# Two-layer diffusion backbone on one core: experts taken in an order set on the chip, 512-wide down and output projections, one closing branch

## The chip, the core and the metric

One NeuronCore of a Trainium2 chip runs the whole program as one launch. TensorE multiplies (PE; its weight loads are PEld), VectorE (DVE) and ScalarE (ACT) do elementwise work, GpSimd (POOL) clears a few tiles, and SyncE (SP) issues every DMA. The metric is the device time of one execution in microseconds; lower is better.

## The reference

Two layers over 256 latent and 256 context tokens of width 1024, all in f32. Each layer normalizes, modulates and projects the tokens, runs three groups of heads (grouped-query attention, a short convolution, differential attention), concatenates them and applies one output projection with a gated residual. Then layer 0 has a dense SwiGLU of width 2816, and layer 1 a mixture of 8 SwiGLU experts of the same width, of which each latent token takes 2:

```python
logits = (h @ rw) + rb
top_v, top_i = lax.top_k(logits, TOP_K)          # 2 of 8
gates = jax.nn.softmax(top_v, axis=-1)
combine = sum(one_hot(top_i, 8) * gates[..., None], axis=-2)
for e in range(8):
    out = out + combine[..., e:e + 1] * swiglu(h, wg[e], wu[e], wd[e])
```

The output is the latent stream after layer 1. The sum over experts can be taken in any order. The weights of one expert are three f32 matrices of 1024 x 2816.

## The kernel before, in words

The program goes through six stages: a first projection, `mixer(0)`, `dense(0)`, `moe_consts` and `route_prep`, `mixer(1)`, `moe(1)`. Up to the experts, an f32 product is made of three fp32r products of a high and a low part (`mm3`, L165); `chunk` (L138) loads a weight block into one of six raw buffers, ACT writes the high part (L148) and DVE the low one (L153). A planner orders the instructions of each engine by priority and readiness; only `pin` and `issue_after` fix an order by hand. Therefore work that stands later in the program can fill gaps of work that stands earlier.

`wo_part` (L694) multiplies half of the output projection (rows 4 to 7 of the mixed heads). It takes the 1024 output columns in four blocks of 256 (`dc`); one PSUM bank of tag "mm" holds two token tiles of 128 next to each other, and `resid2` (L731) multiplies by the gate and adds to the residual. The other half, `tail` (L719), already takes 512 columns at a time.

`dense` (L738) takes the 2816 columns in groups of 10, 10 and 2 blocks of 128. After the gate and up products of a group, the down product (L797) runs: for the two groups of 10 it also takes four blocks of 256 output columns with two "mm" banks, and for the last group it uses `tail`. `side` (L747) takes steps of `ada_next`, a generator that sums the next layer's modulation on DVE from 512 KB loads (L203, L210): four steps ahead of most gate/up pairs, two ahead of each block `dc`, and all that are left ahead of the last group's tail.

`route` (L832) makes the logits, the rank of each expert for a token, the position of each token within its expert (`posm`), the gates (`comb`) and two numbers in `cnt`: the largest count of tokens, and a bit mask of the experts that have more than 64 tokens. `moe` (L903) then goes through experts 0 to 7 in this order. An expert has up to 96 token slots (`CAP`), in three tiles of 32. `gather` (L966) picks the tokens of one or two experts with a permutation made from `posm`; `gate_up` (L1022) and `down` (L1071) go over the 2816 columns in groups of 1024, 1024 and 768; the 32-column products sit side by side in the array (`quads`). The products for the third tile of 32 stand in `third(m)` (L1019), a branch that PE takes only where the mask has the bit of this expert. `spread` adds the expert's result to `acc`.

The weights come through a ring of 14 buffers of 1 MiB (`load`, L934). `plan` (L921) lists the loads: for each group 8 loads for gate and up, and 4 or 3 for the down rows of the group before. Each `fetch` hands out the oldest buffer and issues the next load, which waits until its buffer has been read. SP keeps eight semaphores for its loads, so that at most eight are under way.

After the last expert, `over` (L1169) holds the largest count. Two branches in a row (L1171) test whether it is above 96 and above 192; each body would handle further slots. With these inputs neither body runs.

Of the kernel before, what the change touches and what calls it, by code (L numbers as in the profile page):

```python
# [18 lines left out]
NL = 256  # L19
# [19 lines left out]
C_ID, C_S0, C_S1, C_RA, C_RC, C_UT, C_IO, C_TM, C_P2, C_N = 0, 128, 256, 384, 640, 768, 896, 1024, 1088, 1096  # L39


def build(tc, x, c, ctx, c_ctx, w_ada, b_ada, norm_mix, norm_ffn, w_in, w_out, a_q_gain, a_k_gain,
# [33 lines left out]
    cnt = base.tile([128, 2], I32, name="cnt")  # L76
# [328 lines left out]
    def mixer(l, fill=(), pre=(None, None)):  # L405
# [282 lines left out]
        def wo(s, ps, k, wh, wl, kk, a, b):  # L688
            for i in range(2):
                ts = slice((2 * s + i) * 128, (2 * s + i) * 128 + 128)  # L690
                mm3(ps[:, i * 256:i * 256 + 256], mTh[:, k, ts], mTl[:, k, ts], wh[:, kk], wl[:, kk],
                    i == 0 and a, i == 1 and b, True)

        def wo_part(k0, kn):  # L694
            for dc in range(4):
                acc = {s: bank("mm") for s in qs}
                wh, wl = chunk(krows(w_out[l], k0, kn, dc * 256, 256))
                for s in qs:
                    for kk in range(kn):
                        wo(s, acc[s], k0 + kk, wh, wl, kk, kk == 0, kk == kn - 1)  # L700
                for s in qs:
                    resid2(s, dc, acc[s].rearrange("p (t n) -> p t n", t=2))
# [16 lines left out]
    def tail(t, a, ws, tag=("mm", "mm")):  # L719
        for dh, wd in enumerate(ws):  # L720
            ps = bank(tag[dh])
            n = len(a) // len(wd)
            for kk, (ah, al) in enumerate(a):
                wh, wl = wd[kk // n]
                mm3(ps, ah, al, wh[:, kk % n], wl[:, kk % n], kk == 0, kk == len(a) - 1)
            tmp = hp.tile([128, 512], F32, name="rtmp", tag="sq", bufs=2)
            dsl = slice(dh * 512, dh * 512 + 512)
            dve.tensor_mul(tmp, ps, gb[:, t // 2, dsl])
            dve.tensor_add(X[t][:, dsl], X[t][:, dsl], tmp)

    def resid2(s, dc, ps):  # L731
        tmp = hp.tile([128, 2, 256], F32, name="rtmp", tag="sq", bufs=2)
        dsl = slice(dc * 256, dc * 256 + 256)
        for i in range(2):
            dve.tensor_mul(tmp[:, i], ps[:, i], gb[:, s, dsl])
            dve.tensor_add(X[2 * s + i][:, dsl], X[2 * s + i][:, dsl], tmp[:, i])

    def dense(l):  # L738
        wg, wu, wd = dense_w_gate[l // 2], dense_w_up[l // 2], dense_w_down[l // 2]
        with tc.tile_pool(name="dp", bufs=1, reuse_waits="tile") as dp:  # L740
# [14 lines left out]
            for gn in (10, 10, 2):  # L755
# [41 lines left out]
                for dc in range(4):  # L797
                    side(ST[2])
                    acc = [bank("mm") for _ in range(2)]
                    for fp in range((gn + 3) // 4):  # L800
                        fn = min(4, gn - 4 * fp)
                        wh, wl = chunk(krows(wd, f0 + 4 * fp, fn, dc * 256, 256))
                        for s in range(2):
                            for i in range(2):
                                ts = slice((2 * s + i) * 128, (2 * s + i) * 128 + 128)
                                for kk in range(fn):
                                    f = 4 * fp + kk
                                    mm3(acc[s][:, i * 256:i * 256 + 256], ath[f][:, ts], atl[f][:, ts], wh[:, kk], wl[:, kk],
                                        i == 0 and f == 0, i == 1 and f == gn - 1, True)
                    for s in range(2):  # L810
                        resid2(s, dc, acc[s].rearrange("p (t n) -> p t n", t=2))
# [20 lines left out]
    def route(l, xnh, xnl, rp, mark):  # L832
# [50 lines left out]
        dve.tensor_add(posm, ps[:, 0:16].rearrange("p (t e) -> p t e", t=2), un)  # L883
        for t in LAT:
            dve.scalar_tensor_tensor(xnl[:, t], X[t], rs[t], xnh[:, t].bitcast(F32), op0=OP.mult, op1=OP.subtract)
        mx = rp.tile([128, 2], F32, name="lmx")
# [9 lines left out]
        cf = rp.tile([128, 2], F32, name="cf")  # L896
        fl = rp.tile([128, NE], F32, name="fl")
        dve.scalar_tensor_tensor(fl, ps[:, 16:24], 64.0, KM[:, C_P2 - C_UT:C_P2 - C_UT + NE], op0=OP.is_gt, op1=OP.mult)
        dve.reduce_sum(cf[:, 1:2], fl, axis=AX.X)
        dve.reduce_max(cf[:, 0:1], ps[:, 16:24], axis=AX.X)  # L900
        dve.tensor_copy(cnt, cf)

    def moe(l):  # L903
# [17 lines left out]
        def plan():  # L921
            prev = None
            for e in range(NE):
                for g in range(3):
                    yield from up_rows(moe_w_gate[m, e], moe_w_up[m, e], g)
                    if prev:
                        yield from down_rows(moe_w_down[m, prev[0]], prev[1])
                    prev = e, g
            yield from down_rows(moe_w_down[m, prev[0]], prev[1])
# [24 lines left out]
        while len(queue) < NR:  # L954
            queue.append(load(next(todo)))

# [163 lines left out]
        def gathers(es_):  # L1120
            perm, gh = gather([col(posm, e) for e in es_], iota)
# [8 lines left out]
        gathers((0, 1))  # L1130
        units = []
        pend = aT = py = qT = None
        for e in range(NE):
            gh = where[e][2]
            for g in range(3):
                def mid(e=e, g=g):
# [8 lines left out]
                    if e % 2 == 1 and e < NE - 1 and g == 0:  # L1145
                        gathers((e + 1, e + 2))
# [9 lines left out]
                if pend:  # L1156
                    down(aT, pend[1], py, fetch, more[e - (pend[1] == 2)])
                    if pend[1] == 2:
                        ys = collect(py)
                        units += [(qT, col(comb, e - 1), ys, t, dh, "tp", e == 1) for dh in range(2) for t in LAT]  # L1160
# [5 lines left out]
        for i, (dh, t) in enumerate(((0, 0), (0, 1), (1, 0), (1, 1))):  # L1166
            spread(qT, col(comb, NE - 1), ys, t, dh, ("mm", "mm", "tp", "tp")[i], False, True)

        over = nc.values_load(cnt[0:1, 0:1], min_val=0, max_val=NL)  # L1169
        for rnd in range(1, (NL + CAP - 1) // CAP):  # L1170
            with tc.If(over > CAP * rnd):  # L1171
                io = mp.tile([128, CAP], F32, name="io", tag="io")
                dve.tensor_scalar(io, iota, float(CAP * rnd), None, op0=OP.add)
                with tc.For_i(0, NE, 1) as e:
                    pc = mp.tile([128, 2, 2], F32, name="pc", tag="pc", bufs=1)
                    dve.tensor_copy(pc[:, :, 0:1], posm[:, :, bass.ds(e, 1)])
                    dve.tensor_copy(pc[:, :, 1:2], comb[:, :, bass.ds(e, 1)])
                    perm, gh = gather([[pc[:, t, 0:1] for t in LAT]] * 2, io)
                    qT = permT(perm, 0)

                    def src(w):
                        return w[m, bass.ds(e, 1)].rearrange("o r n -> (o r) n")

                    def rows(parts):
                        it = iter(parts)
                        return lambda: load(next(it))

                    py = [bank("at"), y2]
                    for g in range(3):
                        sg = gate_up(gh[:, 0], g, rows(up_rows(src(moe_w_gate), src(moe_w_up), g)), None, lambda: None)  # L1190
                        down(turn(sg, g), g, py, rows(down_rows(src(moe_w_down), g)))
                    ys = collect(py)
                    for dh in range(2):
                        for t in LAT:
# [121 lines left out]
```

## Time and profile before

| | us |
|---|---|
| three runs | 1583.59, 1584.4, 1586.29 (median 1584.4) |
| profiled execution | 1584.25 |
| its span, first to last instruction | 1582.5 |
| PE busy / weight loads / DVE / ACT | 1486.6 / 994.2 / 700.1 / 486.1 |
| bytes read from HBM | 392.21 MB, 249 GB/s over the span |

The span is what the trace shows; the execution's own time is 1.75 us longer. PE is busy for 94% of the span, but this is an average over stages that have different limits. The span is cut into 40 slices of 39.6 us in one part of the page; the experts' stage begins near 870 us, in the 22nd of them counted from 0.

### The profile page before, as it was taken

How to read it: one execution, taken by the hardware profiler on the slowest of the kernel's cores; microseconds unless marked ns; L12 is line 12 of the kernel's file. 1: busy time of each engine (PE TensorE's matmuls, PEld its weight loads, DVE VectorE, ACT ScalarE, POOL GpSimd, SP SyncE). 2: the span in 40 equal slices, each digit the busy share in tenths (PEclk: the TensorE clock that was granted, in tenths of full speed). 3: DMA queues.
4: the chain of work that ended last, by engine and by line, in shares of the span. 5: the costliest groups of instructions: out<-in, count | busy, mean ns of one | idle time of the engine just before them, and what ended most of it. 6: DMA issues, size and time to landing. Idle time of an engine off the chain costs nothing. (4 is left out here: it accounts for less than half of the span.)

```text
span 1582.5 us, 31693 instructions
## 1 busy us (share of the span) xinstructions
PE 1486.6 (94%) x13286; PEld 994.2 (63%) x13286; DVE 700.1 (44%) x1670; ACT 486.1 (31%) x1067; POOL 2.9 (0%) x17
## 2 busy tenths in 40 slices
PE   8999999999999999999998999999988899999995
PEld 6987767887898889878877354444432344344343
DVE  4798745798377754378866012021202121020222
ACT  4576663533223231366773111010201010010101
POOL 0000000000000000000000000000000000000000
PEclk9999999999999999999998999999999999999997
DMA  9443324267256742324417999999999999999960
GB/s 322 144 133 108 108 67 134 69 200 224 69 169 213 261 135 87 107 64 132 126 41 280 415 416 415 415 416 403 417 407 416 405 416 406 417 373 399 399 242 30
DMA packets 175188, 395.64 MB, mean 250 GB/s; under 512 B 13840, under 2 KB 92588, under 8 KB 175024
## 3 DMA queue, kind: packets, MB, share of 16 engines
q1 hardware_dynamic: 175024, 393.30, 67.0%
q8 instruction: 122, 2.00, 0.5%
q14 instruction: 42, 0.34, 0.1%
HBM read 392.21 MB, written 1.05 MB: 249 GB/s over the span
## 5 line engine op out<-in xcount | busy, mean ns | idle before, releaser
L1005 PE MATMUL mm<-w,gh 128*32 128x512 f32 (+1 forms) x3072 | 327.5, 559 | 18.0 <-DMA w<-in_moe_w_up 13.3
L1005 PEld LDWEIGHTS mm<-w,gh 128*32 128x32 f32 x3072 | 102.8, 110 | 210.8 <-issue 185.1
L1005 PE MATMUL at<-w,aT 128*32 128x256 f32 x3520 | 202.4, 380 | 12.7 <-DMA w<-in_moe_w_down 8.8
L148 ACT CAST w<-w 128x512 fp32r<-128x512 f32 (+1 forms) x244 | 138.4, 605 | 204.9 <-PE mm L167 86.5
L153 DVE TENSOR_TENSOR w<-w 128x1024 fp32r<-128x1024 f32 (+1 forms) x122 | 144.7, 1186 | 92.6 <-ACT w L148 92.4
L1005 PEld LDWEIGHTS at<-w,aT 128*32 128x32 f32 x3520 | 118.9, 110 | 100.3 <-DMA w<-in_moe_w_down 19.4
L166 PE MATMUL mm<-w,hTh 128*128 128x256 f32 (+1 forms) x360 | 107.2, 299 | 3.0 <-ACT hTh L361 2.7
L167 PE MATMUL mm<-w,hTl 128*128 128x256 f32 (+1 forms) x360 | 107.0, 297 | 0.0
L168 PE MATMUL mm<-w,hTh 128*128 128x256 f32 (+1 forms) x360 | 106.5, 296 | 0.0
L166 PE MATMUL mm<-w,aTh 128*128 128x256 f32 (+1 forms) x336 | 97.4, 290 | 0.0
L167 PE MATMUL mm<-w,aTl 128*128 128x256 f32 (+1 forms) x336 | 96.9, 289 | 0.0
L168 PE MATMUL mm<-w,aTh 128*128 128x256 f32 (+1 forms) x336 | 96.7, 288 | 0.0
L1052 DVE COPY aT<-tp 128x256 f32<-128x256 f32 x16 | 6.8, 424 | 174.2 <-PE tp L1051 174.2
L1005 PE MATMUL av<-w,gh 128*32 128x512 f32 (+1 forms) x768 | 81.1, 557 | 0.0
L166 PEld LDWEIGHTS mm<-w,hTh 128*128 128x128 f32 x360 | 69.1, 192 | 7.7 <-ACT hTh L361 3.5
L167 PEld LDWEIGHTS mm<-w,hTl 128*128 128x128 f32 x360 | 69.3, 193 | 4.1 <-issue 2.0
L166 PE MATMUL at<-hTh,w 128*128 128x512 f32 (+1 forms) x192 | 71.3, 373 | 0.3 <-ACT hTh L361 0.3
L168 PEld LDWEIGHTS mm<-w,hTh 128*128 128x128 f32 x360 | 69.1, 192 | 3.8 <-issue 2.4
L167 PE MATMUL at<-hTh,w 128*128 128x512 f32 (+1 forms) x192 | 71.0, 371 | 0.0
L168 PE MATMUL at<-hTl,w 128*128 128x512 f32 (+1 forms) x192 | 71.0, 374 | 0.0
L1041 DVE TENSOR_TENSOR msg<-msg,av 128x256 f32<-128x256 f32 (+1 forms) x24 | 9.6, 399 | 137.5 <-ACT msg L1040 137.5
L1068 DVE COPY aT<-tp 64x256 f32<-64x256 f32 x8 | 3.4, 428 | 149.1 <-ACT aT L1066 149.1
(373 smaller groups left out, 2529.2 us busy)
## 6 DMA issues: line engine op xcount, KB each, us to landing
w<-in_moe_w_down SPq DMA_DIRECT2D x88, 1024.0 KB, 12.2
w<-in_moe_w_gate SPq DMA_DIRECT2D x128, 512.0 KB, 10.8
w<-in_moe_w_up SPq DMA_DIRECT2D x128, 512.0 KB, 10.2
araw<-in_w_ada SPq DMA_DIRECT2D x80, 512.0 KB, 4.3
w<-in_moe_w_gate SPq DMA_DIRECT2D x64, 384.0 KB, 7.9
w<-in_moe_w_up SPq DMA_DIRECT2D x64, 384.0 KB, 7.7
w<-in_w_in SPq DMA_DIRECT2D x36, 512.0 KB, 4.0
w<-in_dense_w_gate SPq DMA_DIRECT2D x22, 512.0 KB, 4.6
```

The costliest lines, as they stand in the source:

```text
L148: act.copy(h[:, sl], r[:, sl])
L153: dve.tensor_sub(lo[:, sl], r[:, sl], h[:, sl].bitcast(F32))
L166: pe.matmul(ps, ah, bh, start=start, stop=False, skip_group_check=shared)
L167: pe.matmul(ps, al, bh, start=False, stop=False, skip_group_check=shared)
L168: return pe.matmul(ps, ah, bl, start=False, stop=stop, skip_group_check=shared)
L1005: pin(pe.matmul(ps(q), lhsT, rhs(q), start=start, stop=stop, tile_position=(0, 32 * q), skip_group_check=True))
L1041: dve.tensor_mul(a, a, ps[t][:, n:2 * n])
L1052: (dve.tensor_copy if c0 else act.copy)(aT[:, c0:c1], pt[:, 0:c1 - c0])
L1068: (dve.tensor_copy, act.copy)[i % 2](at[64:128, 4 * i:hi], pv[64:128, 0:hi - 4 * i, :, 1])
```

## The change

1. `route` also ranks the experts by their count of tokens. 1000 is added to the count of expert 0, so that it has rank 0. Position p of the new order takes the expert whose rank is entry p of 0, 1, 7, 2, 6, 3, 5, 4. The ids, the counts, the positions and the gates are moved into this order with a one-hot matrix (`Pi`), and the bit mask follows it.
2. SP loads the seven ids of positions 1 to 7 into registers after the first 14 loads of the ring, and the addresses of all weight loads from position 1 on are made from them. Position 0 keeps its fixed address.
3. Tokens are gathered for positions (0), (1, 2), (3, 4), (5, 6), (7) rather than in four pairs.
4. `wo_part` and the dense down product of the groups of 10 take 512 output columns at a time, one PSUM bank for each token tile (tags "mm", "mm", "av", "ad"), two weight rows of 512 in a chunk, and `resid` on 512 columns.
5. The second closing branch stands inside the first one.

```diff
-                    yield from up_rows(moe_w_gate[m, e], moe_w_up[m, e], g)
+                    yield from up_rows(at_(moe_w_gate, e), at_(moe_w_up, e), g)
...
+        ids = [0]
+        def at_(w, e):
+            return w[m, 0] if e == 0 else w[m, bass.ds(ids[e], 1)].rearrange("o r n -> (o r) n")
...
         while len(queue) < NR:
             queue.append(load(next(todo)))
+        ids += [nc.values_load(cnt[0:1, 2 + p:3 + p], engines=[mybir.EngineType.SP], min_val=0, max_val=NE - 1)
+                for p in range(1, NE)]
...
+        C = rp.tile([128, NE], F32, name="C")
+        dve.tensor_add(C, ps[:, 16:24], kc(C_K0))
+        o, sl = C[:, None, :].to_broadcast([128, NE, NE]), C[:, :, None].to_broadcast([128, NE, NE])
+        dve.tensor_tensor(g2, o, sl, op=OP.is_gt)
+        dve.tensor_tensor(e2, o, sl, op=OP.is_equal)
+        dve.tensor_mul(e2, e2, TM)
+        dve.tensor_add(g2, g2, e2)
+        dve.reduce_sum(rk, g2, axis=AX.X)
+        dve.tensor_tensor(Pi, rk[:, None, :].to_broadcast([128, NE, NE]), kc(C_OR)[:, :, None].to_broadcast([128, NE, NE]),
+                          op=OP.is_equal)
+        def moved(dst, src):
+            tmp = rp.tile([128, NE, NE], F32, name="tmp", tag="tmp", bufs=2)
+            dve.tensor_mul(tmp, Pi, src[:, None, :].to_broadcast([128, NE, NE]))
+            dve.reduce_sum(dst, tmp, axis=AX.X)
...
+        moved(cf[:, 2:2 + NE], kc(C_EI))
+        dve.tensor_copy(fl, ps[:, 16:24])
+        moved(c2, fl)
+        dve.scalar_tensor_tensor(fl, c2, 64.0, kc(C_P2), op0=OP.is_gt, op1=OP.mult)
...
+        for t in LAT:
+            moved(posm2[:, t], posm[:, t])
...
+        for t in LAT:
+            moved(comb2[:, t], comb[:, t])
...
+    K[:, C_OR:C_OR + NE] = np.array([0, 1, 7, 2, 6, 3, 5, 4])[None]
...
-        gathers((0, 1))
+        gathers((0,))
...
-                    if e % 2 == 1 and e < NE - 1 and g == 0:
-                        gathers((e + 1, e + 2))
+                    if e % 2 == 0 and e < NE - 1 and g == (1 if e == 0 else 0):
+                        gathers((e + 1, e + 2) if e + 2 < NE else (e + 1,))
...
-                for dc in range(4):
+                for dh in range(2):
                     side(ST[2])
-                    acc = [bank("mm") for _ in range(2)]
-                    for fp in range((gn + 3) // 4):
-                        fn = min(4, gn - 4 * fp)
-                        wh, wl = chunk(krows(wd, f0 + 4 * fp, fn, dc * 256, 256))
...
+                    acc = [bank(tag) for tag in ("mm", "mm", "av", "ad")]
+                    for fp in range(gn // 2):
+                        wh, wl = chunk(krows(wd, f0 + 2 * fp, 2, dh * 512, 512))
+                        for t in range(4):
+                            ts = slice(t * 128, t * 128 + 128)
+                            for kk in range(2):
+                                f = 2 * fp + kk
+                                mm3(acc[t], ath[f][:, ts], atl[f][:, ts], wh[:, kk], wl[:, kk], f == 0, f == gn - 1)
+                    for t in range(4):
+                        resid(t, dh, acc[t])
...
+            for dh in range(2):
+                acc = [bank(tag) for tag in ("mm", "mm", "av", "ad")[0:len(qt)]]
+                for kp in range(kn // 2):
+                    wh, wl = chunk(krows(w_out[l], k0 + 2 * kp, 2, dh * 512, 512))
...
+    def resid(t, dh, ps):
+        tmp = hp.tile([128, 512], F32, name="rtmp", tag="sq", bufs=2)
+        dsl = slice(dh * 512, dh * 512 + 512)
+        dve.tensor_mul(tmp, ps, gb[:, t // 2, dsl])
+        dve.tensor_add(X[t][:, dsl], X[t][:, dsl], tmp)
...
-        for rnd in range(1, (NL + CAP - 1) // CAP):
-            with tc.If(over > CAP * rnd):
...
+        with tc.If(over > CAP):
+            further(1)
+            with tc.If(over > 2 * CAP):
+                further(2)
```

## Rows read from the trace of the kernel before

**Rows 1.** The page: bytes moved by DMA, in 40 slices of the span.
```profile
GB/s 322 144 133 108 108 67 134 69 200 224 69 169 213 261 135 87 107 64 132 126 41 280 415 416 415 415 416 403 417 407 416 405 416 406 417 373 399 399 242 30
```

**Rows 2.** Stretches: span, busy us (instructions) by engine, clock, DMA share, GB/s.
```profile
870.00:930.20 60.20, 57.11 (x656) 25.25 (x659) 5.18 (x13) 6.62 (x14) 0.15 (x1) 1.00 1.03 415
930.20:1025.70 95.50, 93.57 (x1127) 45.16 (x1123) 14.84 (x34) 11.23 (x27) 0.15 (x1) 1.00 1.03 416
1025.70:1096.40 70.70, 67.07 (x820) 31.85 (x813) 12.21 (x26) 9.18 (x23) 0.15 (x1) 1.00 1.02 409
1096.40:1180.60 84.20, 72.36 (x805) 31.30 (x803) 14.84 (x34) 11.23 (x27) 0.15 (x1) 1.00 1.02 412
1180.60:1265.00 84.40, 69.33 (x769) 26.76 (x769) 12.22 (x26) 9.19 (x23) 0.15 (x1) 1.00 1.02 411
1265.00:1362.60 97.60, 94.22 (x1124) 43.34 (x1128) 14.12 (x30) 11.23 (x27) 0.15 (x1) 1.00 1.03 412
1362.60:1459.00 96.40, 93.45 (x1144) 40.04 (x1140) 12.21 (x26) 10.35 (x25) 0.15 (x1) 1.00 0.99 392
1459.00:1561.00 102.00, 100.36 (x1290) 44.63 (x1282) 18.69 (x36) 10.85 (x28) 0.15 (x1) 1.00 0.69 268
```

**Rows 3.** The same stretches, instructions on tile av alone (PE, PEld, DVE, ACT).
```profile
930.20:1025.70 95.50, 20.63 (x192) 7.27 (x192) 1.20 (x3) 1.10 (x3) 1.00 1.03 416
1096.40:1180.60 84.20, 0.00 (x0) 0.00 (x0) 1.20 (x3) 1.10 (x3) 1.00 1.02 412
```

**Rows 4.** The chain that ended last: start us, us, what; its last products.
```profile
1552.92 8.04 PE at L1005 x144
```

**Rows 5.** Timeline of SP: start us, us, engine, line, what.
```profile
552.62 5.90 SPq L203 DMA_DIRECT2D araw<-in_w_ada  x2
...
873.40 0.33 SPq L941 DMA_DIRECT2D w<-in_moe_w_up  x1
877.25 0.33 SPq L941 DMA_DIRECT2D w<-in_moe_w_gate  x1
...
1510.23 17.69 SPq L941 DMA_DIRECT2D w<-in_moe_w_down  x7
```

**Rows 6.** DMA issues: what, count, KB each, median us from issue to landing.
```profile
w<-in_moe_w_gate SPq DMA_DIRECT2D x128, 512.0 KB, 10.8
...
araw<-in_w_ada SPq DMA_DIRECT2D x80, 512.0 KB, 4.3
```

**Rows 7.** The closing branches (line 1171): count, ns min/median/max, first and last start.
```profile
L1171 SPq EVENT_SEMAPHORE  x16: 17/17/17, 1573.8 to 1581.1; - x16
...
L1171 PEldq COMPARE_BRANCH  x2: 4285/4690/5094, 1566.4 to 1570.9; - x2
...
L1171 SPq COMPARE_BRANCH  x2: 50/52/53, 1570.8 to 1576.0; - x2
```

**Rows 8.** Stretches as in Rows 2: down products 256 wide, gate/up products 512 wide.
```profile
588.90:646.40 57.50, 57.50 (x481) 57.50 (x480) 23.23 (x40) 12.93 (x25) 0.00 (x0) 1.00 0.32 94
545.40:588.90 43.50, 43.50 (x194) 36.02 (x192) 25.32 (x32) 14.56 (x27) 0.00 (x0) 1.00 0.49 160
```

**Rows 9.** Groups by line: count, busy us, mean ns; a 512-wide eviction on DVE.
```profile
L728 DVE TENSOR_TENSOR rtmp<-mm,gb 128x512 f32<-128x512 f32 x14 | 9.5, 685 | 2.4 <-PE mm L168 2.3
```

**Rows 10.** Timeline of DVE, then of PE, at the end of the routing.
```profile
862.65 0.16 DVE L901 CAST cnt<-cf 128x2 int32<-128x2 f32 x1
862.72 1.34 DVE L972 TENSOR_SCALAR perm<-KM,posm 128x96 fp32r<-128x96 f32 x7
...
863.87 0.50 PE L982 MATMUL tp<-perm,xnh 128*128 128x192 f32 x1 [2.31 <-DVE perm L972]
...
870.03 7.07 PE L1005 MATMUL mm<-w,gh 128*32 128x512 f32 x64
```

**Rows 11.** SP loading one value of cnt into a register at line 1169 (ns).
```profile
L1169 SPq TENSOR_LOAD <-cnt x1: 478/478/478, 1528.0 to 1528.0; - x1
L1169 SPq FUSED_REGOPS  x1: 183/183/183, 1528.5 to 1528.5; - x1
```

More of the change, by code (lines that the diff above doesn't have):

```diff
@@ L75, in build @@
     comb = base.tile([128, 2, NE], F32, name="comb")
[L76 removed]
+    cnt = base.tile([128, 2 + NE], I32, name="cnt")
+    posm2 = base.tile([128, 2, NE], F32, name="posm2")
+    comb2 = base.tile([128, 2, NE], F32, name="comb2")
     hps = ExitStack()
@@ L725, in tail @@
                 mm3(ps, ah, al, wh[:, kk % n], wl[:, kk % n], kk == 0, kk == len(a) - 1)
[L726 to L736, printed above, removed]
+            resid(t, dh, ps)
+    def resid(t, dh, ps):
[3 more added lines that the diff above has]
+        dve.tensor_add(X[t][:, dsl], X[t][:, dsl], tmp)
     def dense(l):
@@ L1120, in gathers @@
         def gathers(es_):
-            perm, gh = gather([col(posm, e) for e in es_], iota)
+            perm, gh = gather([col(posm2 if e else posm, e) for e in es_], iota)
             for i, e in enumerate(es_):
@@ L1166, in moe @@
         for i, (dh, t) in enumerate(((0, 0), (0, 1), (1, 0), (1, 1))):
-            spread(qT, col(comb, NE - 1), ys, t, dh, ("mm", "mm", "tp", "tp")[i], False, True)
+            spread(qT, col(comb2, NE - 1), ys, t, dh, ("mm", "mm", "tp", "tp")[i], False, True)
         over = nc.values_load(cnt[0:1, 0:1], min_val=0, max_val=NL)
-        for rnd in range(1, (NL + CAP - 1) // CAP):
-            with tc.If(over > CAP * rnd):
[L1172 to L1194, printed above, removed]
-                            spread(qT, [pc[:, t, 1:2] for t in LAT], ys, t, dh, "tp", False, True)
@@ new lines, in further, with src, rows @@
+        def further(rnd):
+            io = mp.tile([128, CAP], F32, name="io", tag="io")
+            dve.tensor_scalar(io, iota, float(CAP * rnd), None, op0=OP.add)
+            with tc.For_i(0, NE, 1) as e:
+                pc = mp.tile([128, 2, 2], F32, name="pc", tag="pc", bufs=1)
+                dve.tensor_copy(pc[:, :, 0:1], posm[:, :, bass.ds(e, 1)])
+                dve.tensor_copy(pc[:, :, 1:2], comb[:, :, bass.ds(e, 1)])
+                perm, gh = gather([[pc[:, t, 0:1] for t in LAT]] * 2, io)
+                qT = permT(perm, 0)
+                def src(w):
+                    return w[m, bass.ds(e, 1)].rearrange("o r n -> (o r) n")
+                def rows(parts):
+                    it = iter(parts)
+                    return lambda: load(next(it))
+                py = [bank("at"), y2]
+                for g in range(3):
+                    sg = gate_up(gh[:, 0], g, rows(up_rows(src(moe_w_gate), src(moe_w_up), g)), None, lambda: None)
+                    down(turn(sg, g), g, py, rows(down_rows(src(moe_w_down), g)))
+                ys = collect(py)
+                for dh in range(2):
+                    for t in LAT:
+                        spread(qT, [pc[:, t, 1:2] for t in LAT], ys, t, dh, "tp", False, True)
```

56 lines of the change are left out of this document (24 added, 32 removed).

## The prediction

> **What bounds the kernel now.** I read the page's DMA line first [rows 1]: up to slice 20 little is moved, from slice 22 on some 415 GB/s nearly without a pause, and only the last slices fall. So the experts' stage, 690 of 1582.5 us, streams weights, and the question is where the stream waits for PE and where PE waits for the stream. For that I cut the stage at the first gate/up product of each expert [rows 2] and asked the same stretches for the tile of the third 32 slots [rows 3]. The reader is to see two kinds of experts. Those with over 1100 PE products have the third tile run (192 products on "av"): 1, 5, 6 and 7, so these have more than 64 tokens. Call them big; 0, 2, 3, 4 are small. Two small ones in a row (3 and 4) take 84.2 and 84.4 us with PE busy for 72.4 and 69.3 at most: the stream sets their time, 84.3 us an expert. The big ones take 95.5 to 102 us with PE busy nearly throughout: PE sets theirs. In the order 0 to 7 the kernel pays for both kinds apart: at 1265 PE has used up every buffer, and then three big experts follow, in which the ring of 14 fills, the stream slows to 392 and 268 GB/s, and its last loads are issued by 1528 [rows 5], while PE works until 1552.92 + 8.04 = 1561.0 [rows 4]. After that come the last evictions, the output and 10 us of closing branches [rows 7].
>
> **The order of experts.** Expert 0 is small and first. Of the other seven, ranks 1 to 4 by count are the big ones 1, 5, 6, 7 in some order, and ranks 5 to 7 the small ones. The table 0, 1, 7, 2, 6, 3, 5, 4 therefore gives small, big, small, big, small, big, small, big, whatever the exact counts. Both partners of such a pair are in the trace already: experts 1 and 2, a big one after a small one and a small one after a big one, with one gather of two experts, took 95.5 + 70.7 = 166.2 us while the stream ran at 416 and 409 GB/s [rows 2]. The stream needs 84.2 + 84.4 = 168.6 for a pair. So PE and stream are level in each pair, and the stream barely bounds it. Position 7 starts, counted from the end of position 0, at 930.2 + 3 x 168.6 = 1436.0 by the stream and at 930.2 + 3 x 166.2 = 1428.8 by PE, to which the gather of positions 1 and 2 is added, since it moves into position 0 (under 6.2 us, from the first gather product to the first weight product [rows 10], half of that at full clock). Counted from the moment in the old run when the stream was the bound, 1265.0 + 168.6 = 1433.6. I take the mean of the stream's two values, 1434.8. Position 7 is big: 102.0 us in the old run, less the third tile in the last down products of the expert ahead of it, which is now small (48 of 144 products in 8.04 us, 2.7 [rows 4]): 99.3. PE ends at 1534.1 instead of 1561.0: 26.9 us gained. The ends are 33 (PE alone, 1428.8) and 18, if near-level pairs stutter by 3 us each.
>
> **The start of the experts.** The ranking puts about 20 small DVE instructions (seven up to `Pi`, two for each of six `moved`, one copy) ahead of the first `perm`, if the planner keeps program order. By the copy of `cnt` and the spacing of `perm` (0.16 and 1.34 / 7 = 0.19 us [rows 10]) that is 3.8 us; behind the waiting first gather products stand PE's mask load and all weight products. Only two `perm` and half the gather columns are needed now, which gives back between nothing and 3 us. So PE starts 0.8 to 4 us late. Does the stream notice? SP issues its last free load at 873.40 and the next one at 877.25, when PE has read the first half [rows 5]; a load lands 10.8 us after its issue [rows 6], so a release that is 4 us late still finds loads under way. The seven register loads sit in the same gap: 7 x (0.478 + 0.183) = 4.6 us [rows 11], from 873.7 to 878.3, 1.1 us past the old issue and ahead of the late one; queued behind them are only loads that wait for PE anyway, and 10 us of loads are in flight. I price the whole start at +1.5 us; its ends are 0 and 6.
>
> **The closing branch.** PE's two branches at the end take 4.3 and 5.1 us [rows 7], and SP, which carries the end, goes through its own branch at 1570.8 and 1576.0 and a row of eight semaphores after each, the last at 1581.1. Nested, the second is skipped with the first body: 1581.1 - 1576.0 = 5.1 us less, with nothing late in its place but the output, which lands during the first. Ends: 4.3 and 5.3. [...]
>
> **The 512-wide products.** A down product of 256 columns takes 57.50 / 480 = 0.1198 us, a product of 512 columns 43.50 / 192 = 0.2266 [rows 8], both with PE never idle. Two narrow ones become a wide one: 0.2396 - 0.2266 = 0.0130 us saved each. The dense groups of 10 have 480 such pairs (2 groups x 4 blocks x 10 rows x 4 token tiles x 3 products, halved): 6.2 us. `wo_part` of layer 0 has 96 pairs, of which a quarter fills waits of the attention: 72 x 0.0130 = 0.9. In layer 1 there are 48, most of them in such waits: 0.2. Chunks keep their size of 1024 columns and feed 24 products of 0.2266 = 5.4 us, so loads and casts stay hidden. Evictions: a tile's product with the gate takes 0.685 us [rows 9], and PE comes back to its bank after three other tiles, 3 x 6 x 0.2266 = 4.1 us; hidden, unless DVE is held up. If that cover fails at the four changes of block, up to 1.5 us each, 6 in all. The banks "av" and "ad" are shared with attention and the modulation, and a wait there could cost `wo_part` some 3 us. `side` loses half its calls among the down products: 8 steps slip behind the last gate/up pair. Placed there, eight loads of 4.3 us [rows 6] with two buffers would take some 17 us of SP's queue, ahead of the last down weights and under 21.8 us of gate/up products (96 x 0.2266). But the trace has the last of these loads issued by 558.5 [rows 5], before the second group's down products even start at 588.9, so the planner runs them ahead. I price it at nothing.
>
> **The sum**, on the profiled execution: -26.9 + 1.5 - 5.1 - 6.2 - 0.9 - 0.2 = -37.8, so the span is 1544.7. With the 1.75 us around it and the 0.15 by which this execution was below the median of 1584.4: 1546.6 us.
>
> **Rivals.**
> (a) The early stages give nothing: bank waits and late evictions eat 7.3 us. 1553.9, and up to 1560 with stalls. For it: "av" and "ad" are single buffers. Against: 4.1 us of cover.
> (b) The order pays half, because pairs that are level on average stutter, or position 0 starts late: 1546.6 + 13 = 1560. For it: only 2.4 us of slack in a pair. Against: 14 buffers of 1 MiB, 35 us of stream at 415 GB/s.
> (c) The 13 ns belong not to the width but to which operand stays in the array (gate/up keeps weights, down keeps tokens): the dense edit gives nothing, 1553.9 as in (a), with no stalls seen. [...]
> (d) Slower than before: addresses from registers make SP's issue the bound. An expert has 24 + 24 + 11 = 59 loads in 84.3 us, 1.43 us for each; now one takes 0.33 [rows 5]. Beyond 1.43, seven experts pay 413 x the excess, and at 1.52 us the whole gain of 37.8 is gone; at 1.6 the time is 1546.6 + 70 = 1617. For it: no load with a register's address ran in this trace. Against: it needs 1.19 us on top, six and a half register operations of 0.183 [rows 11].
>
> **How the numbers follow.** The forecast 0.62, (a) 0.12, (b) 0.13, (c) 0.05, (d) 0.05, and 0.03 for a larger gain. The low end takes PE's bound for position 7 (6 us) and a free start (1.5) with a little more: 1538. The high end holds (a), (b) and (c) with some stall: 1565. Within 0.2%, about 3 us, is what a measurement cannot tell from no change; only a mild (d) ends there: 0.01. Faster 0.94, slower 0.05.
>
> **What would show it.** After: big and small stretches alternate, each pair near 168 us, the stream at 410 GB/s until near 1500, position 7 begun about 27 us earlier than the old expert 7; one far branch of PE at the end; no idle time of PE at the block changes of dense down, and its two groups 54.4 us long. SP's issue over 1 us, or PE waiting for loads in big stretches, would make the prediction wrong.

## The result, and the profile after

The changed kernel takes 1562.9 us (1561.6 to 1567.8, 4 runs) where the kernel before takes 1584.0 beside it: a ratio of 0.987, with 0.9846 to 0.9895 as its 95% interval. The profiled execution has a span of 1560.5 us. The forecast was 1546.6, with a span of 1544.7: of the 37.8 us forecast, 22.0 came and 15.8 did not. The time lies inside the stated range of 1538 to 1565, near its high end.

The page of the changed kernel: bytes moved by DMA in 40 slices of the span (answers [rows 1]).
```profile
GB/s 323 148 129 106 121 55 148 68 199 209 92 100 183 239 253 111 98 61 135 131 55 212 398 406 408 404 408 401 408 394 408 400 406 406 396 408 401 408 399 103
```
The experts' stage is even to the last slice, as the order should make it. But it is even at some 405, where the kernel before ran at 415.

The changed kernel by position in the order, cut at the first gate/up product of each; columns as in [rows 2].
```profile
865.15:930.25 65.10, 62.47 (x688) 33.48 (x690) 7.34 (x20) 8.39 (x18) 0.15 (x1) 0.97 1.02 400
930.25:1020.53 90.28, 88.80 (x1092) 39.20 (x1088) 12.22 (x26) 9.18 (x23) 0.15 (x1) 1.00 1.03 406
1020.53:1097.18 76.65, 71.97 (x853) 35.35 (x849) 14.83 (x34) 11.23 (x27) 0.15 (x1) 1.00 1.03 404
1097.18:1188.36 91.18, 89.18 (x1091) 39.39 (x1087) 12.22 (x26) 9.19 (x23) 0.15 (x1) 1.00 1.02 402
1188.36:1267.89 79.53, 72.39 (x853) 34.33 (x846) 14.48 (x32) 11.23 (x27) 0.15 (x1) 1.00 1.02 403
1267.89:1361.24 93.35, 89.57 (x1088) 40.22 (x1092) 12.22 (x26) 9.18 (x23) 0.15 (x1) 1.00 1.02 402
1361.24:1444.81 83.57, 77.34 (x856) 40.03 (x852) 13.72 (x30) 12.09 (x29) 0.15 (x1) 0.96 1.03 405
1444.81:1544.80 99.99, 98.26 (x1246) 44.58 (x1238) 18.66 (x35) 10.83 (x28) 0.15 (x1) 1.00 0.86 338
```
Big and small alternate. The DMA share is 1.02 to 1.03, as in [rows 2]: the DMA engines are no less busy, they move 2% less. The three pairs take 166.9, 170.7 and 176.9 us, where the sum had 168.6 each. Position 1 begins at 930.25, as the second expert of the kernel before did (930.2). Position 7 begins at 1444.8; the sum on record, with its early terms, puts it at 1434.8 - 7.3 + 1.5 = 1429.0. That is where the 15.8 us are: the last position (100.0 for 99.3) and the end (15.7 us from the last down product to the end of the span, 16.4 forecast) cancel. So two signs that the prediction named are missing: the stream at 410 GB/s, and position 7 some 27 us ahead of the old expert 7 (1459.0), where 14.2 came.

The two groups of dense down products in the changed kernel, as stretches (answers [rows 8]).
```profile
416.63:471.03 54.40, 54.40 (x241) 45.05 (x240) 21.42 (x25) 11.96 (x22) 0.00 (x0) 1.00 0.33 99
583.21:637.63 54.42, 54.42 (x242) 45.06 (x241) 25.83 (x32) 13.54 (x25) 0.00 (x0) 1.00 0.36 113
```
54.4 us each and PE never idle, as forecast. The products that count the router's choice ran at 861.3 before and at 853.3 now: the early stages gave 8.0 us (7.3 forecast).

The changed kernel from the router's counts to the first weight product: the timeline of DVE, that of PE (these answer [rows 10]; ahead of them the line of the kernel before for the same counts), and PE's load of the third-tile mask in the view of its line: ns min/median/max, first and last start.
```profile
854.49 0.26 DVE L1000 TENSOR_SCALAR perm<-KM,posm 128x96 fp32r<-128x96 f32 x1
854.88 0.25 DVE L1000 TENSOR_SCALAR perm<-KM,posm 128x96 fp32r<-128x96 f32 x1
...
856.96 0.16 DVE L908 CAST cnt<-cf 128x10 int32<-128x10 f32 x1
```
```profile
861.39 0.17 PE L880 MATMUL at<-selb,ones 128*128 128x8 bf16 x1
```
```profile
853.43 0.17 PE L872 MATMUL at<-selb,ones 128*128 128x8 bf16 x1
858.18 0.42 PE L1010 MATMUL tp<-perm,xnh 128*128 128x96 f32 x1 [4.59 <-DVE tmp L894]
...
865.15 1.08 PE L1033 MATMUL mm<-w,gh 128*32 128x512 f32 x4
```
```profile
L1153 PEldq TENSOR_LOAD <-cnt x1: 491/491/491, 857.2 to 857.2; - x1
```
Both selections of position 0 are ready at 855.13, but PE begins at 858.18. Between them stands PE's load of `cnt`, and `cnt` comes late in the ranking: its copy ends at 857.12.

SP's loads in the changed kernel, fixed and register addresses together: min/median/max ns.
```profile
L967 SPq DMA_DIRECT2D w<-in_moe_w_gate x192: 327/333/1537, 824.6 to 1504.9; - x192
...
L982 SPq TENSOR_LOAD <-cnt x7: 263/271/482, 866.4 to 870.0; - x7
```
An issue takes 0.333 us at the median, 0.328 before; a register address adds a register operation of 0.046 us and a move of 0.029 to it, far from the 1.19 that rival (d) needs. The seven register loads are over by 870.6.

The closing branch in the changed kernel, in the same form (answers [rows 7]).
```profile
L1223 SPq EVENT_SEMAPHORE  x8: 17/17/17, 1557.9 to 1559.1; - x8
...
L1223 PEldq COMPARE_BRANCH  x1: 4127/4127/4127, 1550.6 to 1550.6; - x1
```
One long branch of PE (4.13 us) and one row of eight semaphores are left, as forecast.

### The profile page after: what moved, and what is told of

The parts are those of the page before. It is cut to its first block, busy times and chain, and to the rows that moved or that the text cites. A ratio compares the mean times of both kernels' runs of the same rounds, so it can differ in the third digit from the quotient of the medians.

```text
span 1560.5 us, 31296 instructions
## 1 busy us (share of the span) xinstructions
PE 1480.3 (95%) x12694; PEld 978.4 (63%) x12694; DVE 698.6 (45%) x1634; ACT 486.4 (31%) x1063; POOL 2.9 (0%) x17
## 5 line engine op out<-in xcount | busy, mean ns | idle before, releaser
L150 ACT CAST w<-w 128x512 fp32r<-128x512 f32 x236 | 137.2, 620 | 182.2 <-PE ad L169 65.9
L155 DVE TENSOR_TENSOR w<-w 128x1024 fp32r<-128x1024 f32 x118 | 144.0, 1220 | 102.3 <-ACT w L150 102.1
L168 PE MATMUL mm<-w,hTh 128*128 128x256 f32 (+1 forms) x296 | 93.0, 316 | 4.9 <-ACT hTh L363 2.7
L169 PE MATMUL mm<-w,hTl 128*128 128x256 f32 (+1 forms) x296 | 92.6, 313 | 0.1
L170 PE MATMUL mm<-w,hTh 128*128 128x256 f32 (+1 forms) x296 | 91.9, 311 | 0.0
L529 DVE TENSOR_REDUCE mx<-at 128x1 f32<-128x512 f32 (+1 forms) x96 | 55.3, 596 | 25.9 <-PE at L565 21.2
L212 DVE SCALAR_TENSOR_TENSOR aacc<-araw,sT,aacc 128x512 f32<-128x512 f32 x84 | 58.5, 745 | 17.3 <-DMA araw<-in_w_ada 17.1
L1080 ACT COPY aT<-tp 128x512 f32<-128x512 f32 x16 | 9.4, 585 | 174.8 <-PE tp L1079 174.8
L531 ACT ACTIVATE P<-at,mx 128x512 f32<-128x512 f32 (+1 forms) x96 | 58.6, 615 | 16.6 <-DVE mx L529 11.4
L168 PEld LDWEIGHTS mm<-w,hTh 128*128 128x128 f32 x296 | 56.9, 193 | 10.5 <-ACT hTh L363 3.3
L168 PE MATMUL tp<-hTh,w 128*128 128x512 f32 x160 | 63.2, 395 | 0.0
```

The lines of the kernel that those rows point to most:

```text
L150: act.copy(h[:, sl], r[:, sl])
L155: dve.tensor_sub(lo[:, sl], r[:, sl], h[:, sl].bitcast(F32))
L168: pe.matmul(ps, ah, bh, start=start, stop=False, skip_group_check=shared)
L169: pe.matmul(ps, al, bh, start=False, stop=False, skip_group_check=shared)
L170: return pe.matmul(ps, ah, bl, start=False, stop=stop, skip_group_check=shared)
L212: dve.scalar_tensor_tensor(acc[:, j, sl], r[:, sl], sT[:, k, s:s + 1], acc[:, j, sl], op0=OP.mult, op1=OP.add)
```

## The experiments

Why does the stream run 2% slower with the DMA engines as busy as before? One theory is that loads by register address are slower. The other comes from the memory map of the built programs: the ranking's new tiles push the ten later ring buffers from byte 96256 of a partition, a multiple of 256, to 94848, 128 past one. (The first four buffers, at 196576, lie 224 past one in both kernels.) Four kernels tell these apart.

**Ten buffers moved back.**
```diff
         xnl = xp.tile([128, 2, D], FR, name="xnl", tag="xnl")
+        xp.tile([128, 160], F32, name="pad", tag="pad")
```


> The changed kernel with one unused tile of 640 bytes a partition in the pool of the router's tiles. Nothing computes with it; it only moves the ten later ring buffers from byte 94848 of a partition (128 past a multiple of 256) to 94208 (a multiple of 256 and 512; before the change it was 96256, a multiple too). Theory placement: the changed kernel's weight stream runs at 402 to 406 GB/s, where the kernel before had 409 to 416, because its writes into the buffers start off a boundary. Then the stream comes back to 410 to 416, the stretch from the first product of position 0 to the first of position 7 falls from 579.7 to about 568 us, and the time from 1562.9 to about 1551. Rival registers: loads whose address comes from a register are slower in themselves; the stream stays at 404 and the time within 2 us of 1562.9.


Measured: ratio 0.9787 (0.9768 to 0.9807), span 1548.7. That kernel by position:
```profile
865.55:930.70 65.15, 62.60 (x687) 33.49 (x690) 7.36 (x20) 8.40 (x18) 0.15 (x1) 0.97 1.01 401
930.70:1020.99 90.29, 88.82 (x1093) 39.25 (x1088) 12.22 (x26) 9.20 (x23) 0.15 (x1) 1.00 1.03 415
1020.99:1097.07 76.08, 71.71 (x850) 35.20 (x845) 14.84 (x34) 11.25 (x27) 0.15 (x1) 1.00 1.02 411
1097.07:1187.56 90.49, 89.02 (x1095) 41.00 (x1091) 12.22 (x26) 9.21 (x23) 0.15 (x1) 1.00 1.02 412
1187.56:1262.84 75.28, 71.34 (x852) 35.75 (x848) 14.49 (x32) 11.25 (x27) 0.15 (x1) 1.00 1.03 413
1262.84:1353.15 90.31, 88.84 (x1092) 39.23 (x1088) 12.22 (x26) 9.20 (x23) 0.15 (x1) 1.00 1.02 407
1353.15:1433.72 80.57, 74.42 (x857) 40.70 (x853) 13.73 (x30) 12.10 (x29) 0.15 (x1) 1.00 1.03 413
1433.72:1533.69 99.97, 98.24 (x1246) 44.54 (x1238) 18.67 (x35) 10.86 (x28) 0.15 (x1) 1.00 0.85 341
```
A tile that nobody uses gives back 11.8 us of span. Position 1 begins as late as without it (930.7), position 7 11.1 us earlier. The gain grows from position 4 on (0.8 us at its start, 5.1 at position 5, 8.1 at 6); PE's share of a small position rises from 91 to 95% (position 4: 72.39 of 79.53, then 71.34 of 75.28).

**All 14 buffers on multiples of 256.**
```diff
+        st.enter_context(tc.tile_pool(name="pad", bufs=1, side="right")).tile([128, 120], F32, name="pad", tag="pad")
         wa = st.enter_context(tc.tile_pool(name="w8a", bufs=1, side="right", reuse_waits="tile"))
...
+        xp.tile([128, 40], F32, name="pad2", tag="pad2")
```


> As the kernel with ten buffers moved, and the four buffers that are filled during attention as well (from byte 196576, which is 224 past a multiple of 256, to 196096, a multiple; they lie off it in the kernel before, too). Theory placement: a further 4 of 14 buffers lose a penalty of some 2%, so the stream gains about 0.6% more, 3 us in 570, until PE sets the time: about 1548. Rival registers: 1562.9 as before. A third case, that only the ten matter: 1551, as the kernel with ten.


Measured: 0.9773 (0.9752 to 0.9793), span 1547.9: not told apart from the kernel with ten. The stream runs at 411 to 417 in positions 1 to 6, for 407 to 415, but position 7 begins only 0.6 us earlier. PE has hardly a wait for weights left to lose (3.9 us in all in the kernel with ten), so PE sets the time by now.

**The kernel before, moved off the boundary.**
```diff
         xnl = xp.tile([128, 2, D], FR, name="xnl", tag="xnl")
+        xp.tile([128, 32], F32, name="pad", tag="pad")
```


> The kernel before, with one unused tile of 128 bytes a partition in the pool of the router's tiles: its ten later ring buffers move from 96256 to 96128, 128 past a multiple of 256, as they lie in the changed kernel. Addresses stay fixed and the experts keep their order. Theory placement: the stream falls from 409..416 to 402..406 GB/s, and experts 0 to 4, which it sets the time of (395 us), take about 8 us more: 1584.0 + 8 = 1592, with 6 to 10 as bounds. Rival registers, and the rival that the order of the experts' addresses slows the stream: no change, 1584 within 2 us.


Measured: 1.0052 (1.0034 to 1.0070), 8 us slower, as expected. Its experts 0 to 4:
```profile
871.83:931.86 60.03, 56.88 (x653) 25.12 (x655) 4.91 (x12) 6.63 (x14) 0.15 (x1) 1.00 1.03 406
931.86:1027.55 95.69, 93.77 (x1128) 45.24 (x1124) 14.84 (x34) 11.25 (x27) 0.15 (x1) 1.00 1.03 407
1027.55:1102.57 75.02, 67.82 (x820) 30.75 (x813) 12.22 (x26) 9.21 (x23) 0.15 (x1) 1.00 1.03 403
1102.57:1188.66 86.09, 72.83 (x801) 31.25 (x802) 14.84 (x34) 11.24 (x27) 0.15 (x1) 1.00 1.02 402
1188.66:1274.62 85.96, 69.50 (x770) 26.59 (x769) 12.22 (x26) 9.20 (x23) 0.15 (x1) 1.00 1.02 402
```
6 to 10 GB/s are gone in each stretch with fixed addresses and the old order, and a small expert after a small one takes 86.0 us for 84.3. The page's queue lines say the same: packets, MB, the time that packets took as a share of 16 engines' span. First the kernel before, then the same with buffers off the boundary:
```profile
q1 hardware_dynamic: 175024, 393.30, 67.0%
```
```profile
q1 hardware_dynamic: 175024, 393.30, 67.3%
```
The same packets cost 0.670 x 1582.5 = 1060 us of all engines' time on the boundary and 0.673 x 1591.5 = 1071 off it.

**The order written into the program**: no ranking, no register.
```diff
-            return w[m, 0] if e == 0 else w[m, bass.ds(ids[e], 1)].rearrange("o r n -> (o r) n")
+            return w[m, EXP[e]]
```


> The changed kernel with the order of the experts written into the program (0, 1, 3, 7, 2, 5, 4, 6, the order that the counts of these inputs give by the table): no ranking, no register loads, fixed addresses. Without the ranking's tiles its ten later buffers come back to 96256, a multiple of 256. Left out is that the order follows the counts of other inputs. Theory placement: the same as the kernel with registers and ten buffers moved, less the ranking in front of the first gather (1.5 us in the sum on record, 0 to 6): 1546 to 1551, stream 410 to 416. Rival registers: the same here, but then the kernel with ten buffers moved stays near 1563 and the two are 12 us apart.


Measured: 0.9803 (0.9779 to 0.9828), span 1547.1, stream 409 to 415. Against 0.9787 with registers: register addresses cost nothing that can be measured. The first weight product comes at 862.8 instead of 865.6 (the ranking's 2.8 us) and position 7 2.9 us earlier, yet the end of the span only 1.6: from the last down product to the end it took 16.4 us for 15.0. These spans are one execution each; the five times of this kernel run from 1548.9 to 1558.8 us.

Next, each part of the change by itself on the kernel before.

**Wide products alone**, the diff's parts in `wo_part`, `resid` and `dense`.
```diff
-                for dc in range(4):
+                for dh in range(2):
...
-                    acc = [bank("mm") for _ in range(2)]
+                    acc = [bank(tag) for tag in ("mm", "mm", "av", "ad")]
```


> The kernel before with the 512-wide down products of the dense layer and of half the output projection, and nothing else of the change. The sum on record has 6.2 + 0.9 + 0.2 = 7.3 us for it; the changed kernel's router counts came 8.0 us earlier (853.35 for 861.3). Theory: the whole start of the experts comes 7.3 to 8 us earlier and all that follows with it: the ratio is 0.995 (1584 - 7.6 = 1576.4). Rival, the stream: the experts wait for weights from the first on, and since the loads start earlier only as buffers come free, part is lost: 0.9975. Rival, operand order: 0.999, with products of 113 ns or more for each 256 columns.


Measured: 0.9956 (0.9938 to 0.9973), 7.0 us. The first weight product is at 861.84 for 870.03, 8.2 us earlier. In the profiled execution, the slowest of the six, 6.3 of these are left when expert 5 begins and 3.8 when the last down product ends (1557.2 for 1561.0); expert 6 alone took 1.6 us longer, at a mean granted clock of 0.98 for 1.00. So the 7.0 us rest on the six times, and that all of it arrives isn't shown.

**The nested branch alone.**
```diff
-        for rnd in range(1, (NL + CAP - 1) // CAP):
-            with tc.If(over > CAP * rnd):
...
+        with tc.If(over > CAP):
+            further(1)
+            with tc.If(over > 2 * CAP):
+                further(2)
```


> The kernel before with the second further round nested inside the first, and nothing else of the change. The sum on record has 5.1 us (4.3 to 5.3); the changed kernel had 5.8 us less between the last product and the end of the span (15.7 for 21.5), with the last expert's combination in both. Theory: PE has one long branch at the end instead of two, and the ratio is 0.9968 (5.1 of 1584). Rival: SP's end hangs on the output's landing and the remaining branch, so only 1 to 2 us are saved, ratio 0.999.


Measured: 0.9971 (0.9961 to 0.9980), 4.6 us. From the last down product to the end of the span it takes 16.6 us for 21.5.

**The order alone**: the ranking, the register addresses and the moved gathers, with the ten buffers aligned.
```diff
+            return w[m, 0] if e == 0 else w[m, bass.ds(ids[e], 1)].rearrange("o r n -> (o r) n")
...
+        gathers((0,))
...
+        xp.tile([128, 160], F32, name="pad", tag="pad")
```


> The kernel before with the order made on the chip and nothing else of the change, its ten later ring buffers at 94208, a multiple of 256. On record the order has -26.9 + 1.5 = -25.4 us, ratio 0.984. In the kernel with ten buffers moved position 1 began at 930.7, as late as in the kernel before (930.0), though the router was 7.6 us earlier: if the ranking (2.3 us), the gather of one expert that takes as long as that of two, and the gather of positions 1 and 2 inside position 0 cost those 8 us, then this kernel's position 1 begins at about 938, PE then works through to 1541 and the time is 1584 - 20 + 1 = 1565, ratio 0.9875. If the start costs only the 1.5 us, position 1 begins at 932 and the ratio is 0.984 or less.


Measured: 0.9874 (0.9856 to 0.9893), 20.0 us. Position 1 begins at 936.5, position 7 at 1440.9, and the last down product ends at 1541.2, as the expectation has it where the start costs those 8 us. The three parts add up: 7.0 + 4.6 + 20.0 = 31.6, and all together, with ten buffers aligned, 0.0213 x 1584 = 33.7 (30.6 to 36.7).

Then the start of the experts.

**Positions 0 and 1 gathered together**, all buffers aligned.
```diff
-        gathers((0,))
+        gathers((0, 1))
...
-                    if e % 2 == 0 and e < NE - 1 and g == (1 if e == 0 else 0):
-                        gathers((e + 1, e + 2) if e + 2 < NE else (e + 1,))
+                    if e % 2 == 1 and e < NE - 1 and g == 0:
+                        gathers((e + 1, e + 2))
```


> The kernel with all 14 ring buffers on multiples of 256, and with positions 0 and 1 gathered together ahead of the first weight product, then 2 and 3, 4 and 5, 6 and 7: four gather calls instead of five. A gather product of 96 columns took 0.21 us, as long as one of 192 in the kernel before, so a call costs the same for one expert as for two. Theory, PE bounds all positions once the buffers are aligned: one call of 32 products less is 3.5 us (at 0.11 us each) to 5 us, less about 1 us that the first call waits longer for the ranking: the ratio falls from 0.9773 by 0.0015 to 0.0025, to about 0.9755. Rival, the stream sets positions 2, 4 and 6: no change, 0.977; rival, the first call waits for the whole ranking: slower than 0.9773 by 0.001.


Measured: 0.9793 (0.9774 to 0.9813): no gain. Position 0 in this kernel, then in the one without the edit:
```profile
867.50:931.45 63.95, 59.83 (x655) 24.65 (x658) 4.92 (x12) 6.62 (x14) 0.15 (x1) 0.97 1.03 417
```
```profile
865.97:930.89 64.92, 62.37 (x687) 33.45 (x690) 7.34 (x20) 8.38 (x18) 0.15 (x1) 0.97 1.02 407
```
The 32 products are gone from position 0, but it shrinks by 1.0 us and not by 3.5. PE is busy for only 2.5 us less (the first ten weight products now take 3.62 us) and idle for 1.6 more. It also begins 1.5 us later, so position 1 comes 0.6 us later, and position 7 2.2 (1435.4 for 1433.2).

**PE's mask load behind the first gather**, all buffers aligned.
```diff
-        big = nc.tensor.value_load(cnt[0:1, 1:2], min_val=0, max_val=2 ** NE - 1)
...
+        gathers((0,))
+        big = nc.tensor.value_load(cnt[0:1, 1:2], min_val=0, max_val=2 ** NE - 1)
         more = [(big >> e) & 1 for e in range(NE)]
-        gathers((0,))
```


> The kernel with all 14 ring buffers on multiples of 256, and PE's load of the third-tile mask moved from ahead of the first gather to behind it. In the changed kernel the first gather's selection was ready at 855.13, but PE's load of the counts, which waits until 857.16 for the whole ranking, stands in front, and the first gather product started at 858.18. Theory, the mask load holds PE and PE bounds every position once the buffers are aligned: the first gather comes 2.5 to 3 us earlier, about 1 us goes back for the load behind it, position 7 and the end come 1.5 to 2.5 us earlier, ratio 0.976 for 0.9773. Rival, the stream bounds a position ahead of position 7 and takes the time back: 0.9773.


Measured: 0.9781 (0.9768 to 0.9794), span 1547.3. PE in that kernel, from the counts to the gather:
```profile
853.20 0.17 PE L872 MATMUL at<-selb,ones 128*128 128x8 bf16 x1
854.67 0.42 PE L1012 MATMUL tp<-perm,xnh 128*128 128x96 f32 x1 [1.31 <-DVE e L884]
```
The gather now starts 1.5 us after the counts instead of 4.8, and position 1 at 927.0 for 930.9: the mask load did hold PE. But position 7 begins only 1.0 us earlier. Position 6 took the rest, first in this kernel, then in the one without the edit:
```profile
1348.94:1432.20 83.26, 77.36 (x856) 41.24 (x852) 13.73 (x30) 12.09 (x29) 0.15 (x1) 0.96 1.03 416
```
```profile
1353.09:1433.16 80.07, 74.22 (x856) 39.33 (x852) 13.73 (x30) 12.08 (x29) 0.15 (x1) 1.00 1.03 415
```
PE was busy 3.1 us longer for the same 856 products, at a mean granted clock of 0.96 for 1.00. So neither theory is borne out: in this execution the lower clock took it, not the stream.

**The mask load late, and 24 products that nobody reads** while PE would wait, all buffers aligned.
```diff
+        def busy(n):
+            for _ in range(n):
+                pin(pe.matmul(warm, xnh[:, 0, 0:128], xnh[:, 0, 0:512], start=True, stop=True))
+        busy(18)
...
         pe.matmul(ps[:, 16:24], ones, selb[:, 1], start=False, stop=True)
+        busy(6)
```


> As the kernel with the mask load moved, and with 24 products of 512 columns that nobody reads, 18 while PE waits for the router's choice and 6 while it waits for the first gather's selection. In the changed kernel the granted clock is 0.50 from 850 to 867, and the first gather (0.213 us a product) and the first weight products run at it. Theory: busy PE keeps the granted clock at 1.00, the gather of 32 products takes 3.5 us instead of 6.9 and the first 64 weight products 7.0 instead of 8.7, so position 1 begins 5 us earlier than with the mask load alone; with PE as the bound all of it reaches the end: ratio 0.973. Rival: the stream then bounds (positions 2, 4, 6 wait for weights) and under 2 us of the 5 are left, 0.975. Rival: the added products delay the router's choice and nothing is gained.


Measured: 0.9763 (0.9749 to 0.9776), span 1544.8, the lowest of all that ran, though inside the interval of the kernel with all buffers aligned. Four stretches; the first weight product is at 860.96:
```profile
850.00:855.00 5.00, 5.00 (x22) 3.80 (x21) 2.81 (x13) 0.00 (x0) 0.00 (x0) 0.71 0.97 379
855.00:860.00 5.00, 4.04 (x33) 3.79 (x31) 4.49 (x32) 1.24 (x3) 0.00 (x0) 0.97 1.03 416
860.00:865.00 5.00, 5.00 (x33) 1.94 (x37) 0.75 (x2) 1.77 (x3) 0.00 (x0) 0.68 1.03 420
865.00:870.00 5.00, 4.14 (x44) 1.04 (x39) 0.00 (x0) 0.22 (x1) 0.00 (x0) 1.00 1.03 416
```
The clock is up for most of the gather, which takes 5.3 us instead of 7.0, and falls again at the gather's end and under the first weight products, though PE was idle for no more than 1 us just before. Position 1 begins at 925.3, 1.7 us earlier than with the mask load alone; 5 were expected. That the added products would keep the clock at 1.00 is refuted.

**Ten buffers on a multiple of 256 that is none of 512.**
```diff
-        xp.tile([128, 160], F32, name="pad", tag="pad")
+        xp.tile([128, 96], F32, name="pad", tag="pad")
```


> The changed kernel with its ten later ring buffers at 94464: a multiple of 256, but not of 512. [...] If a coarser boundary counts (512 or more), it stays at the changed kernel's 0.987 and 404 GB/s, or lies between.


Measured: 0.9782 (0.9765 to 0.9800), span 1548.7, position 7 at 1434.0: as with the multiple of 512, so 512 isn't the boundary that counts here. Its positions 1 and 4:
```profile
930.85:1021.16 90.31, 88.84 (x1092) 39.22 (x1088) 12.22 (x26) 9.18 (x23) 0.15 (x1) 1.00 1.03 415
1187.77:1263.07 75.30, 71.35 (x852) 35.74 (x848) 14.48 (x32) 11.23 (x27) 0.15 (x1) 1.00 1.02 410
```
Five places of the ten buffers have now been run: 96256, 94464 and 94208, multiples of 256, are fast, and 94848 and 96128, 128 past one, are slow. Other offsets of these ten weren't run.

**The early start with the buffers where the changed kernel has them**: the two edits above without the pads.
```diff
-        st.enter_context(tc.tile_pool(name="pad", bufs=1, side="right")).tile([128, 120], F32, name="pad", tag="pad")
...
-        xp.tile([128, 40], F32, name="pad2", tag="pad2")
```


> The changed kernel with its buffers where it has them (94848, off the boundary), the mask load moved and the 24 products added. Theory, in the changed kernel the stream sets the start of position 7 and not PE: starting the experts earlier by 5 to 7 us gains at most what the loads start earlier, under 2 us, ratio 0.986 to 0.987. Rival, PE's late start is what the changed kernel lacked: ratio 0.983.


Measured: 0.9852 (0.9838 to 0.9865), beside 0.987 for the changed kernel: no difference that can be told. Position 1 begins 2.0 us earlier than in the changed kernel (928.3), position 5 0.4 later (1268.3), the last down product ends at 1544.0 for 1544.8. Its positions 6 and 7, and PE's waits for one kind of load: us in total, times, longest.
```profile
1360.91:1440.32 79.41, 74.07 (x856) 38.82 (x849) 13.73 (x30) 12.08 (x29) 0.15 (x1) 1.00 1.02 405
1440.32:1543.96 103.64, 99.28 (x1242) 43.45 (x1242) 18.67 (x35) 10.84 (x28) 0.15 (x1) 1.00 0.87 344
```
```profile
PE mm L1041 <- DMA w<-in_moe_w_up: 3.1, 6, 0.6
```
Position 7 begins 4.5 us earlier than in the changed kernel, but PE then waits 3.1 us for weights, all six times in position 7, where the changed kernel has no such wait. Off the boundary the stream takes an early start back, as expected. Beside the kernel with the same two edits and all buffers aligned, the pads alone are worth 0.9852 - 0.9763 = 0.0089, 14.1 us.

## Why the prediction missed its point

**The stream's rate was taken as fixed (the failing step).** "The stream needs 84.2 + 84.4 = 168.6 for a pair" carried the rate of [rows 2] over to a kernel with other buffer addresses. The rate follows the buffers: 402 to 406 GB/s in positions 1 to 6 of the changed kernel, 128 bytes past a multiple of 256, for 407 to 415 on one, and 402 to 407 in experts 0 to 4 of the kernel before when moved off it, for 409 to 416. So it does in either order and with either kind of address. Over seven positions that is 11.8 of the 15.8 us, by the one kernel that differs in an unused tile; the mirror image on the kernel before costs 8 us. Some 3 us of the 11.8 arose in position 6, where the changed kernel also had its clock at 0.50 for a while (below); the kernel off the boundary with the early start has no such dip there, begins position 7 earlier and waits for weights instead: 183.1 us for positions 6 and 7, the changed one 183.6. So off the boundary the stream sets the two together, with the dip or without. None of the rivals named the buffers' place. That the time still lies inside the range is luck: the range was wide for the causes of rivals (a) to (c).

Why 128 bytes past a multiple of 256 costs the stream 2% isn't shown: the runs moved only the buffers, the written side, and show the rate that followed.

**The start of the experts: +1.5 forecast (0 to 6 as its ends), 8.3 paid.** In the kernel with ten aligned buffers the counts came 7.6 us early (853.7) and position 1 0.7 late (930.7 for 930.0, the first single product; [rows 2] cuts at 930.2). (i) The forecast put PE's mask load "behind the waiting first gather products"; it stands ahead, and waits for the whole ranking: 4.8 us from counts to gather for 2.5, +2.3. (ii) Half the gather columns were to give back up to 3 us; they gave -0.8: 32 products of 96 columns took 6.96 us, all at a clock of 0.50, and 32 of 192 took 6.16, the last 8 of them at 1.00. (iii) The gather of positions 1 and 2 inside position 0, and its first 64 weight products in 8.7 us for 7.1, make position 0 5.2 us longer. The argument that 10 us of loads in flight cover a late PE looked at the stream alone; once the stream keeps its rate, PE is the bound from position 1 on, and a late start is carried on: the fixed order began 2.8 us earlier, and its position 7 2.9. With that the sum closes. Position 1 comes 7.5 us after the 923.2 that the sum implies (1429.0 less three pairs of 168.6). The three pairs from there take 503.0 us, 2.8 less, the last position 0.7 more and the end 1.4 less: 4.0 us, the rest of the 15.8.

**What held.** The order: aligned, its pairs take 166.4, 165.8 and 170.9 us, for 168.6 by the stream and 166.2 by PE. The wide products: 54.4 us a group, 7.0 us alone for 7.3. The branch: 4.6 alone, for 5.1. Rival (c) is out by the 54.4; rival (d) by issues of 0.333 us and by the fixed order. Rival (a) is out by the 8.0 us of the early stages. Rival (b) named nearly the right time, 1560. Of its two causes the runs refute one, as level pairs don't stutter on the boundary; the other, a late start, came true for part of the loss.

## What to carry to other kernels

In these runs the stream's rate belonged to its buffers' addresses too: before carrying a rate over a change that adds tiles, compare where the buffers begin, modulo 256 bytes, and pad if needed; here 640 unused bytes a partition were worth more than half of the order (11.8 us of span for 20.0). Once a change makes two bounds level, a delay that the old bound would have hidden is paid (the fixed order's 2.8 us at the start were 2.9 at position 7), so the start of the stage has to be costed on both, PE and the stream, with the order of register loads read off the engine's own timeline.

## What the runs showed that I had not expected

Gather products of 96 and of 192 columns take the same: 0.21 us each at a granted clock of 0.50, and 0.11 at 1.00, as their starts in the timelines show. Halving their columns saved nothing here.

The clock was at 0.50 through the routing's end in both kernels, and rose at 869 in both, but the changed kernel's weight products had begun by then, at 865.15. Its stretches:
```profile
865.15:868.70 3.55, 3.55 (x21) 0.93 (x24) 0.38 (x1) 1.71 (x2) 0.00 (x0) 0.50 1.03 411
868.70:873.97 5.27, 5.26 (x52) 1.26 (x44) 0.00 (x0) 0.00 (x0) 0.00 (x0) 1.00 1.03 410
```
And it fell to 0.50 once more in position 6, at the end of a gather and with the gate's products (L306) next, with PE busy for 6.12 of 6.80 us:
```profile
1361.24:1373.90 12.66, 12.02 (x108) 6.37 (x100) 1.83 (x5) 2.20 (x6) 0.00 (x0) 1.00 1.03 407
1373.90:1380.70 6.80, 6.12 (x17) 1.92 (x16) 0.75 (x2) 1.64 (x4) 0.00 (x0) 0.50 1.03 410
```
At the same place the profiled executions of the order alone and of the two aligned kernels with the mask load late show it too (these two have 0.96 over position 6). So does that of the wide products alone, in expert 6 from about 1371, with no gather ahead of the gate's products; the one with the early start off the boundary shows a short one near 1097 instead (0.99 over position 3). The other aligned versions of the changed kernel don't (1.00 over position 6 in four of them). Position 6 or expert 6 took 1.1 to 3.2 us longer with it. It can differ between executions of one kernel: with the fixed order the mean granted clock of the five was 0.984 to 0.988, the two lowest took 1557.0 and 1558.8 us, the highest 1548.9. What sets it off stays open.
